# Side matmuls tied behind the main product in front of them, and the scans' three blocks in one burst

## The chip, the cores and the metric

The kernel runs on one core of one Trainium2 chip. The metric is the device time of one execution in microseconds (us); the time before is the median of 3 runs. TensorE (PE) multiplies and writes PSUM, VectorE (DVE) and ScalarE (ACT) do the elementwise work, GpSimd (POOL) issues small loads and clears tiles, SyncE (SP) issues the weight loads.

## The reference, cut to what matters

Two streams of 128 tokens (a prompt and a sample) go through two layers of a hybrid transformer block of width 2048. Only the parts around the change are kept here.

```python
def _mixer(h, p, ctx):
    u = h @ p['w_in']
    q, k, v, u_hy, u_rkv, w_dn, a_dn, g_dn = jnp.split(u, IN_SPLITS, axis=-1)
    att = attention(q, k, v)             # 12 heads, 4 kv heads; the sample also sees a cached context
    hy = _hyena(u_hy, p)                 # long convolution by FFT
    rw, S_fin = _rwkv(u_rkv, w_dn, a_dn, g_dn, p, S0)
    return concat([att, hy, rw]) @ p['w_out']

def _layer(x, cond, p, ctx):
    sh1, sc1, g1, sh2, sc2, g2 = silu(cond) @ ada_w + ada_b
    x = x + g1 * rmsnorm(_mixer(rmsnorm(x) * (1 + sc1) + sh1))
    h = rmsnorm(x) * (1 + sc2) + sh2
    return x + g2 * rmsnorm(square(relu(h @ p['mlp_w1'])) @ p['mlp_w2'])

def step(S, inp):                        # _rwkv: a scan over the 128 tokens, both directions, 12 heads
    sk = S @ kk_t
    S = S * w_t - outer(sk, kk_t * a_t) + outer(v_t, k_t)
    return S, S @ r_t
```

## The kernel before, in words

**Main products.** `ws` (L481) and `as_` (L503) multiply activations by weights streamed from HBM. `wload` (L211) loads a weight tile by SP, rounds it to a high part on ACT (L219) and takes the rest as a low part on DVE (L220); there are four raw tiles and three of each part. Each product is three matmuls (high by high, high by low, low by high): L495, L498, L499 in `ws`, L514, L517, L518 in `as_`. Both are generators and yield once for each k-step (128 rows of the weight), with the count of columns they streamed.

**Side work.** Attention, the hyena convolution and the RWKV recurrence are generators that `Side` holds. `run` (L1089) drives a main product: after each k-step it adds columns/6144 to `side.now` (0.5 for a 512-wide product, 0.375 for a 384-wide one), gives each generator credit at its rate, and lets a generator run on to its next yield when it has a whole credit and the number that it yielded last has passed on `side.now`. So the program text interleaves k-steps and side steps; `drain` runs what is left when an output needs it. The vectors of the adaptive modulation (`ada_vector`, L361, matmuls L374) are a third stream, driven by `ada_step`.

**Order on the engines.** The tile framework reorders: it dispatches each engine's instructions by program order among those that are ready in its own model of time. An engine then works through its queue strictly in that order. A side matmul whose turn in the program comes after a main product may thus stand ahead of it in PE's queue, where the model held the product's weights to be late.

**Attention** (L647) for each stream: transposes of keys (L686) and queries (L693), scores (L705), softmax on DVE and ACT (L708 to L718), transposes of the probabilities (L725), products with the values (L734). It yields 0.5 and `wa1` = 1.5 after its two halves of the scores, before the transposes. Its generator has the rate `ra` = 0.3. **Hyena** (L598): transposes (L612), spectra (L619, L620), and for each of four channel groups four matmuls back (L639, L640) and a yield.

**RWKV** works on 6 blocks of 128 channels in 2 batches of 3. A batch builds triangular matrices for each block (`rwkv_stage1`), sends their diagonal pieces through HBM (L937, L938, read back by SP at L956), inverts all at once by 30 steps on DVE (L964, L965; `rwkv_invert`), and then solves by blocks of 32 tokens in `rwkv_stage2` (L980): seven steps, alternately with the inverted diagonal (L1003) and with what lies off it (L1001). Each step does, for each of the three channel blocks in turn, 8 matmuls into one PSUM tile `sm`, two evictions (L1007, or L1009 and L1011) and a yield of `w5` = 0.25. There are three `sm` tiles for all side work.

Of the kernel before, what the change touches and what calls it, by code (L numbers as in the profile page):

```python
# [33 lines left out]
def _shape_constants():  # L34
# [56 lines left out]
    for k, v in c.items():  # L91
# [18 lines left out]
            ni=3, w2=0.5, w3=3, w4=2, w5=0.25, fill=8, b1=2, b2=5)  # L110
# [46 lines left out]

class Kern:
    def __init__(self, tc, es, A, O, opts=None):
# [6 lines left out]
        self.side = Side()  # L166
        self.adaq = deque()
# [56 lines left out]
    def setup(self):  # L224
# [17 lines left out]
        nc.tensor.transpose(ps[:, 0:32], th[:], self.ident[0:32, 0:32])  # L242
# [21 lines left out]
    def params(self, l):  # L264
# [34 lines left out]
        for i, gr in enumerate(groups):  # L299
# [3 lines left out]
            nc.tensor.transpose(ps[:, 0:n], rows[:], self.ident[0:n, 0:n])  # L303
# [151 lines left out]
    def norm(self, P, parts, isc, ish, act):  # L455
# [3 lines left out]
        for c in range(4):  # L459
            for g in range(2):  # L460
# [4 lines left out]
                for j in range(4):  # L465
                    nc.tensor.transpose(pv[:, j, :], xn[:, j * 128:(j + 1) * 128], self.ident)
# [14 lines left out]
    def ws(self, act, w, widths, ps):  # L481
# [21 lines left out]
    def as_(self, lhs, ks, w, ncol, ps):  # L503
# [3 lines left out]
        for i0 in range(0, len(ks), nk):  # L507
            hi, lo = self.wload(w[ks[i0] * 128:(ks[i0] + nk) * 128, :], nk, ncol)
            for kk in range(nk):
                first, last = i0 + kk == 0, i0 + kk == len(ks) - 1  # L510
                for g in range(2):
                    hh, hl = (a[:, g * 128:(g + 1) * 128] for a in lhs[ks[i0 + kk]])
                    o = ps[:, g * 512:g * 512 + ncol]
                    m = nc.tensor.matmul(o, lhsT=hh, rhs=hi[:, kk, :], start=first, stop=False)  # L514
# [35 lines left out]
    def hyena_filter(self, l):  # L550
# [16 lines left out]
        nc.tensor.matmul(ps[0:64, 0:128], lhsT=f1[:], rhs=self.cst("featt")[0:33, :], start=True, stop=True)  # L567
# [3 lines left out]
        nc.tensor.matmul(ps[0:64, 0:128], lhsT=f2[:], rhs=h1[:], start=True, stop=True)  # L571
# [5 lines left out]
        for q in range(2):  # L577
            ps = self.sm()
            nc.tensor.matmul(ps[:], lhsT=h2[:], rhs=f3[:, q * 512:(q + 1) * 512], start=True, stop=True)
            nc.vector.scalar_tensor_tensor(h[:, q * 512:(q + 1) * 512], dec[:, q * 512:(q + 1) * 512], 0.05, ps[:], op0=ALU.add, op1=ALU.mult)  # L580
            yield
# [8 lines left out]
        for i, (m, src) in enumerate((("cosm", hs), ("sinm", hd), ("cosn", hs))):  # L590
            ps = self.sm()
            nc.tensor.matmul(ps[:], lhsT=self.cst(m), rhs=src[:], start=True, stop=True)
# [5 lines left out]
    def hyena(self, l, P, hy):  # L598
# [11 lines left out]
        for j in range(4):  # L610
            for g in range(2):
                nc.tensor.transpose(pz[g][:, j * 128:(j + 1) * 128], z[j][:, g, :], self.ident)  # L612
            yield
        Y = []
        for g in range(2):
# [3 lines left out]
            nc.tensor.matmul(pa[:], lhsT=self.cst("cosm"), rhs=zt[:], start=True, stop=True)  # L619
            nc.tensor.matmul(pb[:], lhsT=self.cst("fb"), rhs=zt[:], start=True, stop=True)  # L620
# [14 lines left out]
        for j in range(4):  # L635
            ps = self.sm()
            for g in range(2):
                o = ps[:, g * 128:(g + 1) * 128]
                nc.tensor.matmul(o, lhsT=Y[g][0][:, j * 128:(j + 1) * 128], rhs=self.cst("ia"), start=True, stop=False)  # L639
                nc.tensor.matmul(o, lhsT=Y[g][1][:, j * 128:(j + 1) * 128], rhs=self.cst("ib"), start=False, stop=True)  # L640
# [6 lines left out]
    def attention(self, l, P, qk, v):  # L647
# [27 lines left out]
        for g in range(2):  # L675
# [7 lines left out]
            for i, kk in enumerate((kd, kc)[:g + 1]):  # L683
                ps = self.sm()
                for n in range(4):
                    nc.tensor.transpose(ps[:, n * 128:(n + 1) * 128], kk[:, n, :, :].rearrange("p r d -> p (r d)"), self.ident)  # L686
# [3 lines left out]
            for h0, hn in ((0, 4), (4, 2)):  # L690
                ps = self.sm()
                for j in range(hn):
                    nc.tensor.transpose(ps[:, j * 128:(j + 1) * 128], src[:, (h0 + j) * 128:(h0 + j + 1) * 128], self.ident)  # L693
# [4 lines left out]
            for b0, hpb in (((0, 4), (4, 2)), ((0, 2), (2, 2), (4, 2)))[g]:  # L698
                pes, pTs = [], []
                for par in range(2):  # L700
# [3 lines left out]
                    for j, h in enumerate(range(NH)[hsl]):  # L704
                        nc.tensor.matmul(ps[:, j * nk:(j + 1) * nk], lhsT=qT[o:o + 64, h // 2, :], rhs=kT[o:o + 64, h // 3, :], start=True, stop=True)  # L705
# [15 lines left out]
                for par in range(2):  # L721
                    ps = self.sm()
                    for j in range(hpb):
                        for i in range(g + 1):
                            nc.tensor.transpose(ps[:, j * nk + i * 128:j * nk + (i + 1) * 128], pes[par][:, j, i * 128:(i + 1) * 128], self.ident)  # L725
# [4 lines left out]
                for j in range(hpb):  # L730
                    for i in range(g + 1):
                        for par in range(2):
                            n = (2 * (b0 + j) + par) // 3
                            nc.tensor.matmul(po[64 * par:64 * par + 64, j * 128:(j + 1) * 128], lhsT=vs[i][:, n * 64:(n + 1) * 64],  # L734
# [37 lines left out]
    def rwkv_state(self, l, P, bt):  # L772
# [7 lines left out]
        for d in range(2):  # L780
            ps = self.sm()
            for b in range(3):
                nc.tensor.transpose(ps[:, b * 64:(b + 1) * 64], s[d][:, 2 * b:2 * b + 2, :].rearrange("p h k -> p (h k)"), self.ident[0:64, 0:64])
# [3 lines left out]
    def rwkv_kk(self, P, bt, k):  # L787
# [3 lines left out]
        for bi in range(3):  # L791
# [3 lines left out]
            nc.tensor.matmul(ps[0:6, 0:256], lhsT=self.cst("ones6")[:, 6 * bi:6 * bi + 6], rhs=sq[:], start=(bi == 0), stop=(bi == 2))  # L795
# [575 lines left out]
```

## Time and profile before

| | us |
|---|---|
| median of 3 runs | 2942.34 |
| the runs | 2932.66 to 2944.27 |
| the profiled execution, its own time | 2951.85 |
| its span, first to last instruction | 2950.1 |
| PE busy in the span | 2840.5 (96%) |
| DVE, ACT busy | 1652.6, 1231.1 |
| mean granted TensorE clock | 0.967 |

How to read the rows below. A row of instructions by line has the line, engine, operation, out<-in with its shape and count, then busy us and mean ns. A row of the timeline has start and duration in us, the engine, line, tiles, shape and the count that was merged; in brackets stands the idle time of the engine before it and what ended it. A matmul of fp32 data is two records in the trace, of the rounded type one. A row of a stretch has its start and end, its length, the busy us of PE, PEld, DVE, ACT and POOL with their counts, then the granted clock (1.00 is 2.4 GHz, 0.50 is 1.2 GHz), the share of the DMA engines that was busy, and GB/s. Matmuls overlap, so the time that one adds is read from the starts, not from the durations.

### The profile page before, as it was taken

The page shows a single profiled execution, that of the slowest core. Times are in us where ns is not written, and L with a number is a line of the kernel's source. Part 1 is how long each engine was busy: PE and PEld are TensorE (multiplying, and loading weights), DVE is VectorE, ACT ScalarE, POOL GpSimd, SP SyncE. Part 2 cuts the span into 40 slices and gives each one's busy share as a digit, 9 for nine tenths or more (in the row PEclk, how much of TensorE's full clock was granted, in tenths as well). Part 3 has the DMA queues.
Part 4 walks back from the last instruction along what each step waited for, and adds up shares of the span by engine and source line. Part 5 has one row for each costly group of instructions (what it writes and reads, how often), then busy time and mean ns, then how long its engine had stood idle before and what let it go on. Part 6 is the DMA issues. An engine that isn't in the chain of part 4 may idle for free.

```text
span 2950.1 us, 47852 instructions
## 1 busy us (share of the span) xinstructions
PE 2840.5 (96%) x19163; PEld 2330.7 (79%) x19163; DVE 1652.6 (56%) x2627; ACT 1231.1 (42%) x1870; POOL 177.7 (6%) x368
## 2 busy tenths in 40 slices
PE   6899999999999999999999999999879999999998
PEld 2586788766798797887876978887669989889896
DVE  1356666777644344444445576776775545555555
ACT  2254345434534343343335454453354444434343
POOL 0011101201000000000001111011000000000000
PEclk8899999999999999999999998997889999999999
DMA  9885575478888888888888744532455666666674
GB/s 341 308 300 195 187 257 158 140 263 282 296 278 293 276 287 274 297 279 280 300 318 274 227 124 124 145 92 88 131 195 164 184 189 186 187 191 186 188 238 153
DMA packets 326057, 654.56 MB, mean 222 GB/s; under 512 B 48581, under 2 KB 86030, under 8 KB 325707
## 3 DMA queue, kind: packets, MB, share of 16 engines
q1 hardware_dynamic: 311328, 610.88, 63.8%
q0 software_dynamic: 12928, 36.98, 3.7%
q10 hardware_dynamic: 1579, 3.64, 0.3%
q8 instruction: 150, 2.46, 0.3%
q14 instruction: 72, 0.59, 0.1%
HBM read 632.21 MB, written 19.20 MB: 221 GB/s over the span
## 4 chain that ended last, share of the span: by engine, by line
PE 86%; DVE 6%; DMA 4%; ACT 2%; issue 2%; SPq 0%; POOL 0%; DVEq 0%; ACTq 0%; POOLq 0%
PE mm L495 13%; PE mm L498 12%; PE mm L499 12%; PE mm L514 11%; PE mm L517 11%; PE mm L518 10%; PE ada L374 5%; PE sm L904 2%; DMA wa<-in_ada_w_dram 1%; PE sm L925 1%; PE sm L1003 1%; DVE wl L220 1%; PE sm L1018 1%; PE sm L1001 1%; DMA wr<-in_ada_w_dram 1%
## 5 line engine op out<-in xcount | busy, mean ns | idle before, releaser
L220 DVE TENSOR_TENSOR wl<-wr,wh 128x1024 fp32r<-128x1024 f32 (+1 forms) x784 | 928.9, 1186 | 929.7 <-ACT wh L219 900.3
L219 ACT CAST wh<-wr 128x1024 fp32r<-128x1024 f32 (+1 forms) x784 | 796.7, 1017 | 1163.2 <-PE mm L498 548.2
L495 PE MATMUL mm<-acth,wh 128*128 128x256 f32 (+1 forms) x3200 | 918.8, 287 | 9.9 <-ACT acth L476 8.3
L498 PE MATMUL mm<-actl,wh 128*128 128x256 f32 (+1 forms) x3200 | 908.5, 284 | 0.0
L499 PE MATMUL mm<-acth,wl 128*128 128x256 f32 (+1 forms) x3200 | 905.3, 283 | 2.4 <-DVE wl L220 2.4
L495 PEld LDWEIGHTS mm<-acth,wh 128*128 128x128 f32 (+1 forms) x3200 | 604.8, 189 | 54.7 <-issue 23.1
L499 PEld LDWEIGHTS mm<-acth,wl 128*128 128x128 f32 (+1 forms) x3200 | 605.6, 189 | 8.3 <-DVE wl L220 3.4
L498 PEld LDWEIGHTS mm<-actl,wh 128*128 128x128 f32 (+1 forms) x3200 | 603.7, 189 | 3.6 <-issue 2.5
L514 PE MATMUL mm<-wh,fh 128*128 128x512 f32 x1024 | 406.0, 396 | 0.0
L517 PE MATMUL mm<-wl,fh 128*128 128x512 f32 x1024 | 403.1, 394 | 0.8 <-DVE wl L220 0.8
L518 PE MATMUL mm<-wh,fl 128*128 128x512 f32 x1024 | 401.7, 392 | 0.0
L514 PEld LDWEIGHTS mm<-wh,fh 128*128 128x128 f32 x1024 | 192.2, 188 | 63.4 <-ACT wh L219 11.4
L518 PEld LDWEIGHTS mm<-wh,fl 128*128 128x128 f32 x1024 | 192.0, 188 | 45.3
L517 PEld LDWEIGHTS mm<-wl,fh 128*128 128x128 f32 x1024 | 192.3, 188 | 43.2 <-DVE wl L220 1.2
L374 PE MATMUL ada<-wa,cs 128*32 128x512 f32 x1280 | 183.1, 610 | 7.3 <-DMA wa<-in_ada_w_dram 7.3
L514 PE MATMUL mm<-wh,osh 128*128 128x512 f32 x256 | 107.9, 422 | 3.4 <-ACT osh L1172 3.4
L517 PE MATMUL mm<-wl,osh 128*128 128x512 f32 x256 | 103.9, 406 | 3.4 <-DVE wl L220 3.4
L518 PE MATMUL mm<-wh,osl 128*128 128x512 f32 x256 | 102.5, 400 | 0.0
L374 PEld LDWEIGHTS ada<-wa,cs 128*32 128x32 f32 x1280 | 35.5, 109 | 83.5 <-issue 55.3
L904 PE MATMUL sm<-rZR,rKB 64*128 64x256 f32 x384 | 82.3, 446 | 1.1 <-ACT rKBt L882 0.5
L514 PE MATMUL mm<-wh,acth 128*128 128x512 f32 (+1 forms) x192 | 74.3, 387 | 0.0
L517 PE MATMUL mm<-wl,acth 128*128 128x512 f32 (+1 forms) x192 | 68.9, 359 | 0.0
(323 smaller groups left out, 2619.5 us busy)
## 6 DMA issues: line engine op xcount, KB each, us to landing
wr<-in_mlp_w_dram SPq DMA_DIRECT2D x512, 512.0 KB
wa<-in_ada_w_dram SPq DMA_DIRECT2D x352, 512.0 KB
wr<-in_w_in_dram SPq DMA_DIRECT2D x96, 512.0 KB
wr<-in_w_in_dram SPq DMA_DIRECT2D x112, 384.0 KB
wr<-in_w_out_dram SPq DMA_DIRECT2D x64, 512.0 KB
wr<-in_ada_w_dram SPq DMA_DIRECT2D x32, 512.0 KB
gb<-gate POOLq DMA_DIRECT2D x16, 512.0 KB, 9.6
xd<-acc SPq DMA_DIRECT2D x24, 256.0 KB
```

The lines of the kernel that those rows point to most:

```text
L219: nc.scalar.copy(hi, raw)
L220: nc.vector.tensor_sub(lo, raw, hi)
L374: nc.tensor.matmul(ps[32 * j:32 * j + 32, :], lhsT=self.cs[:, kk, :], rhs=w[2 * (kk - k + 1) + j // 2][:, 512 * (j % 2):512 * (j % 2) + 51 ...
L495: m = nc.tensor.matmul(o, lhsT=h, rhs=hh, start=(k == 0 and b % 2 == 0), stop=False, skip_group_check=True)
L498: nc.tensor.matmul(o, lhsT=h, rhs=hl, start=False, stop=False, skip_group_check=True)
L499: nc.tensor.matmul(o, lhsT=lw, rhs=hh, start=False, stop=(k == KT - 1), skip_group_check=True)
L514: m = nc.tensor.matmul(o, lhsT=hh, rhs=hi[:, kk, :], start=first, stop=False)
L517: nc.tensor.matmul(o, lhsT=hh, rhs=lo[:, kk, :], start=False, stop=False)
L518: nc.tensor.matmul(o, lhsT=hl, rhs=hi[:, kk, :], start=False, stop=last)
L904: nc.tensor.matmul(ps[h][:, i * 256:(i + 1) * 256], lhsT=KB[hs, d, g, i, :], rhs=ZR[hs, d, g, :, :].rearrange("p i t -> p (i t)"), start=T ...
L925: nc.tensor.matmul(o[:, 64 * h:64 * h + 64], lhsT=R.MA[d][h][:, 0:128] if i == 0 else MY[h][:], rhs=vT[:, g, 64 * h:64 * h + 64], start=fi ...
L1001: nc.tensor.matmul(o, lhsT=LA[d][:, gh, qs[d]], rhs=G[:, d, gh, :], start=True, stop=True)
```

## The change

Two edits. First, a class `Beside`: `ws` and `as_` issue the first matmul of each product (L495, L514) through `te.main`, which keeps its name. Every matmul and transpose of the side work, of the norms and of the small setup steps (not those of the modulation, L335, L344, L374, L398) goes through `te.matmul` or `te.transpose`, which adds an edge without a semaphore: the instruction may not be placed ahead of that last main matmul in PE's queue. Second, in the solve each step first takes three `sm` tiles, issues the 24 matmuls of the three blocks, then the six evictions, and yields once, 3 x `w5`, with `w5` 0.4 in place of 0.25.

```diff
-            ni=3, w2=0.5, w3=3, w4=2, w5=0.25, fill=8, b1=2, b2=5)
+            ni=3, w2=0.5, w3=3, w4=2, w5=0.4, fill=8, b1=2, b2=5)
+class Beside:
+    def __init__(self, tc):
+        self.tc, self.last = tc, None
+    def main(self, *a, **k):
+        i = self.tc.nc.tensor.matmul(*a, **k)
+        self.last = i.ins.name
+        return i
+    def queue(self, i):
+        if self.last is not None:
+            self.tc.add_manual_dep(i.ins, self.last, mybir.DependencyInfo(mybir.DependencyClass.NoSync, mybir.DependencyReason.DATA),
+                                   reason="beside")
+        return i
+    def matmul(self, *a, **k):
+        return self.queue(self.tc.nc.tensor.matmul(*a, **k))
+    def transpose(self, *a, **k):
+        return self.queue(self.tc.nc.tensor.transpose(*a, **k))
...
-                    m = nc.tensor.matmul(o, lhsT=h, rhs=hh, start=(k == 0 and b % 2 == 0), stop=False, skip_group_check=True)
+                    m = self.te.main(o, lhsT=h, rhs=hh, start=(k == 0 and b % 2 == 0), stop=False, skip_group_check=True)
...
-                        nc.tensor.matmul(ps[:, j * nk:(j + 1) * nk], lhsT=qT[o:o + 64, h // 2, :], rhs=kT[o:o + 64, h // 3, :], start=True, stop=True)
+                        self.te.matmul(ps[:, j * nk:(j + 1) * nk], lhsT=qT[o:o + 64, h // 2, :], rhs=kT[o:o + 64, h // 3, :], start=True, stop=True)
...
             for first in (True, False)[it == 0:]:
+
+                pss = [self.sm() for b in B]
                 for bi, b in enumerate(B):
                     vT, KBt, G, Y, bv, LA = P.st[b]
-                    ps = self.sm()
                     for gh in range(4):
                         for d in range(2):
-                            o = ps[qs[d], gh * 64:(gh + 1) * 64]
+                            o = pss[bi][qs[d], gh * 64:(gh + 1) * 64]
...
+                for bi, b in enumerate(B):
+                    G = P.st[b][2]
                     for d in range(2):
-                        v = ps[qs[d], 0:256].rearrange("p (i v) -> p i v", i=4)
+                        v = pss[bi][qs[d], 0:256].rearrange("p (i v) -> p i v", i=4)
...
-                    yield self.o["w5"]
+                yield 3 * self.o["w5"]
```

## Rows read from the trace of the kernel before

**Rows 1.** The page, part 1: busy time of each engine.
```profile
PE 2840.5 (96%) x19163; PEld 2330.7 (79%) x19163; DVE 1652.6 (56%) x2627; ACT 1231.1 (42%) x1870; POOL 177.7 (6%) x368
```
**Rows 2.** The page, part 4: the chain that ended last, by engine.
```profile
PE 86%; DVE 6%; DMA 4%; ACT 2%; issue 2%; SPq 0%; POOL 0%; DVEq 0%; ACTq 0%; POOLq 0%
```
**Rows 3.** Timeline of PE, layer 0, around the prompt's attention.
```profile
333.92 0.60 PE L686 MATMUL sm<-const,akd 128*128 128x128 f32 x4
...
342.07 0.99 PE L725 MATMUL sm<-const,ape 128*128 128x128 f32 x4 [2.99 <-DVE ape L718]
...
349.58 0.58 PE L495 MATMUL mm<-acth,wh 128*128 128x256 f32 x1
...
351.21 0.58 PE L499 MATMUL mm<-acth,wl 128*128 128x256 f32 x1 [0.84 <-DVE wl L220]
```
**Rows 4.** Stretches: that detour in each layer, and the main products after the first.
```profile
333.92:349.58 15.66, 10.98 (x69) 7.73 (x67) 8.80 (x33) 7.72 (x28) 0.00 (x0) 0.77 0.10 41
1802.71:1818.84 16.13, 11.06 (x61) 8.49 (x59) 10.23 (x36) 7.52 (x27) 0.00 (x0) 0.62 0.00 1
349.58:356.10 6.52, 5.68 (x26) 5.39 (x26) 6.24 (x17) 2.09 (x4) 0.94 (x1) 0.51 0.52 156
```
**Rows 5.** Timeline of ACT in the same place.
```profile
334.56 0.59 ACT L687 COPY akT<-sm 128x512 f32<-128x512 f32 x1 [8.16 <-PE sm L686]
...
347.66 0.81 ACT L219 CAST wh<-wr 128x768 fp32r<-128x768 f32 x1
```
**Rows 6.** Timeline of SP's queue in the same place.
```profile
329.65 0.42 SPq L369 DMA_DIRECT2D wa<-in_ada_w_dram  x1
351.18 1.44 SPq L218 DMA_DIRECT2D wr<-in_w_in_dram  x2
```
**Rows 7.** Timeline of PE, layer 1: the transposes where main products stand between them.
```profile
1860.60 0.53 PE L725 MATMUL sm<-const,ape 128*128 128x128 f32 x2 [0.86 <-DVE ape L718]
```
**Rows 8.** Timeline of PE and DVE, layer 1, around the hyena products.
```profile
2067.36 0.48 PE L514 MATMUL mm<-wh,osh 128*128 128x512 f32 x1
2070.82 0.50 PE L517 MATMUL mm<-wl,osh 128*128 128x512 f32 x1 [2.97 <-DVE wl L220]
...
2066.46 0.19 DVE L964 TENSOR_TENSOR rkt<-rX 112x30 f32<-112x30 f32 x1
...
2069.55 1.22 DVE L220 TENSOR_TENSOR wl<-wr,wh 128x1024 fp32r<-128x1024 f32 x1
```
**Rows 9.** Stretches: those hyena products with the wait, and the scan's slow part.
```profile
2064.65:2070.82 6.17, 3.20 (x27) 2.84 (x25) 5.76 (x17) 3.91 (x5) 0.00 (x0) 1.00 0.00 0
2110.50:2130.90 20.40, 18.97 (x162) 13.18 (x162) 6.13 (x14) 2.86 (x6) 0.00 (x0) 0.50 0.25 71
```
**Rows 10.** Groups by line: the scans' matmuls and evictions, half of the inversion.
```profile
L1003 PE MATMUL sm<-rG,rXT 32*32 32x64 f32 x768 | 33.6, 228 | 2.0 <-DMA rXT<-rdout 2.0
L1001 PE MATMUL sm<-rG,rLA 128*32 128x64 f32 x576 | 24.3, 229 | 0.6 <-DVE rG L1007 0.6
L1007 DVE TENSOR_TENSOR rG<-rG,sm 32x256 f32<-32x256 f32 x72 | 30.0, 417 | 15.9 <-PE sm L1001 14.3
L965 DVE TENSOR_TENSOR rX<-rX,rkt 112x30 f32<-112x30 f32 (+14 forms) x120 | 39.6, 330 | 2.9
```
**Rows 11.** Timeline of PE: one scan block alone (layer 1), two in one (layer 0).
```profile
2145.36 0.64 PE L1001 MATMUL sm<-rG,rLA 128*32 128x64 f32 x16
...
2146.27 0.39 PE L517 MATMUL mm<-wl,osh 128*128 128x512 f32 x1
2146.50 0.40 PE L518 MATMUL mm<-wh,osl 128*128 128x512 f32 x1
...
2147.51 0.64 PE L1001 MATMUL sm<-rG,rLA 128*32 128x64 f32 x16
...
671.51 1.08 PE L1003 MATMUL sm<-rG,rXT 32*32 32x64 f32 x32
672.52 1.05 PE L374 MATMUL ada<-wa,cs 128*32 128x512 f32 x2
```

More of the change, by code (lines that the diff above doesn't have):

```diff
@@ L166, in __init__ @@
         self.side = Side()
+        self.te = Beside(tc)
         self.adaq = deque()
@@ L241, in setup @@
         ps = self.sm()
-        nc.tensor.transpose(ps[:, 0:32], th[:], self.ident[0:32, 0:32])
+        self.te.transpose(ps[:, 0:32], th[:], self.ident[0:32, 0:32])
         nc.vector.tensor_copy(self.cs[:, :, 0:2], ps[:, 0:32].rearrange("p (c k) -> p k c", c=2))
@@ L302, in params @@
             ps = self.sm()
-            nc.tensor.transpose(ps[:, 0:n], rows[:], self.ident[0:n, 0:n])
+            self.te.transpose(ps[:, 0:n], rows[:], self.ident[0:n, 0:n])
             pv = sb([128, n], F32, tag=f"pv{i}", bufs=2)
@@ L513, in as_ @@
                     o = ps[:, g * 512:g * 512 + ncol]
-                    m = nc.tensor.matmul(o, lhsT=hh, rhs=hi[:, kk, :], start=first, stop=False)
+                    m = self.te.main(o, lhsT=hh, rhs=hi[:, kk, :], start=first, stop=False)
                     if g == 0 and kk == 0:
@@ L591, in hyena_filter @@
             ps = self.sm()
-            nc.tensor.matmul(ps[:], lhsT=self.cst(m), rhs=src[:], start=True, stop=True)
+            self.te.matmul(ps[:], lhsT=self.cst(m), rhs=src[:], start=True, stop=True)
             H = sb([128, 512], F32, tag="hHs")
@@ L611, in hyena @@
             for g in range(2):
-                nc.tensor.transpose(pz[g][:, j * 128:(j + 1) * 128], z[j][:, g, :], self.ident)
+                self.te.transpose(pz[g][:, j * 128:(j + 1) * 128], z[j][:, g, :], self.ident)
             yield
@@ L618, in hyena @@
             pa, pb = self.sm(), self.sm()
-            nc.tensor.matmul(pa[:], lhsT=self.cst("cosm"), rhs=zt[:], start=True, stop=True)
-            nc.tensor.matmul(pb[:], lhsT=self.cst("fb"), rhs=zt[:], start=True, stop=True)
+            self.te.matmul(pa[:], lhsT=self.cst("cosm"), rhs=zt[:], start=True, stop=True)
+            self.te.matmul(pb[:], lhsT=self.cst("fb"), rhs=zt[:], start=True, stop=True)
             ya = sb([128, 512], F32, tag="hya")
@@ L813, in rwkv_stage1 @@
         for g in range(2):
-            nc.tensor.transpose(ps[:, g * 128:(g + 1) * 128], v[:, g, :], self.ident)
+            self.te.transpose(ps[:, g * 128:(g + 1) * 128], v[:, g, :], self.ident)
         vT = sb([128, 2, 128], F32, tag="rvT")
@@ L921, in rwkv_stage1 @@
                     if g == 1:
-                        nc.tensor.matmul(o, lhsT=ZR[:, d, 1, i, :], rhs=S0[:, d, :, :].rearrange("p h v -> p (h v)"), start=first, stop=False, skip_group_check=True)
+                        self.te.matmul(o, lhsT=ZR[:, d, 1, i, :], rhs=S0[:, d, :, :].rearrange("p h v -> p (h v)"), start=first, stop=False, skip_group_check=True)
                         first = False
                     for h in range(0 if (i, d) == (1, 0) else 2):
-                        nc.tensor.matmul(o[:, 64 * h:64 * h + 64], lhsT=R.MA[d][h][:, 0:128] if i == 0 else MY[h][:], rhs=vT[:, g, 64 * h:64 * h + 64],
+                        self.te.matmul(o[:, 64 * h:64 * h + 64], lhsT=R.MA[d][h][:, 0:128] if i == 0 else MY[h][:], rhs=vT[:, g, 64 * h:64 * h + 64],
                                          start=first, stop=True, skip_group_check=True)
```

52 lines of the change are left out of this document (26 added, 26 removed).

## The prediction

> **What bounds the kernel now.** The page comes first: PE is busy for 96% of the span, DVE for 56% and ACT for 42% [rows 1], and 86% of the chain that ended last is PE's [rows 2]. So time falls only where PE does less, where it waits less, or where its clock stays up. In the MLPs I found no PE idle time that this change touches. So I went through PE's timeline in the two mixers, and looked where side matmuls stand in a row with no main product between them.
>
> The clearest place is the prompt's attention, once in each layer. Its generator yields 0.5 and 1.5 between scores and transposes, and a k-step of a 384-wide product counts 0.375, so in the program two and four k-steps belong there. In PE's queue there is none: transposes, scores, transposes and value products stand together from 333.92 to 349.58, and PE waits there, longest for the softmax (2.99 us) [rows 3]. Layer 1 has the same from 1802.71 on [rows 4]. Were the weights of the overtaken products really late? In both stretches the DMA engines are nearly idle, at 0.10 and 0.00 [rows 4]. SP issues its last load at 329.65 and the next one at 351.18 [rows 6]: the raw tiles are full. ACT sat idle for 8.16 us until the first key transposes came, then worked on attention, and took up the next weight cast only at 347.66 [rows 5]. So the weights lay there; ACT's queue, in the order that follows PE's, stood before their cast. The granted clock falls to a mean of 0.77 and 0.62 in these stretches and is 0.51 for the main products behind the first [rows 4]. **That detour is the main thing to be won.**
>
> **Part 1, the order of the queue.** The edges carry no semaphore, so no engine gets a new wait from them. Only the place in PE's queue changes. No DMA is tied, and nothing is moved past one on SP's or POOL's queue by the edge itself; the softmax and the evictions on DVE and ACT go along because they read these matmuls.
>
> Attention, layer 0. The detour takes 15.66 us, of which PE is busy for 10.98 [rows 4]. At a mean clock of 0.77 some 46% of the stretch, 7.2 us, is at half speed, and nearly all of it is busy time after 342 [rows 3], so half of it, about 3.3 us, is the clock's. The work itself is 7.7 us. Cut into about six pieces among main products it pays for switching: 0.2 us each, worked out for the scans below, so 6 x 0.2 = 1.2 us. Saved: 15.66 - 7.7 - 1.2 = 6.8 us. Behind it the main products run for 6.5 us at half clock and lose 0.84 us to a late low part [rows 3, 4]; that is (6.5 - 0.84) / 2 + 0.84 = 3.7 us. Together 10.5 us. Layer 1, same steps: 16.13 us, 11.06 busy, three quarters of the stretch at half clock (0.62), so work of 6.5 us and switching of 1 us, saved 8.6 us, and some 2.4 us behind it: 11 us. Sum 21.5 us. Against it, the softmax latency does not vanish: where transposes already stand among main products PE still waited 0.86 us [rows 7]. I put two such waits on each layer, and take off 4 us. **Term: -17.5 us**, bounds -21.5 (no new wait) and -12 (every idle us of the detours, 4.7 and 5.1, comes back elsewhere).
>
> Hyena. Here the side work is a filler. From 2064.65 to 2067.36 PE does products of several channel groups with no k-step between, then L514, then waits 2.97 us for a low part [rows 8], because DVE works on the inversion from 2066.46 and splits the weights only at 2069.55 [rows 8]. Behind the edge these 2.7 us come after the wait, so PE stands still for almost all of 6.17 us, where its idle time is now 2.97 us [rows 9]. Layer 0 has half of it (two channel groups, about 1.8 us at the price of these). After so long a pause I expect the clock to fall; the nearest row of a fall, 20.4 us at 0.50 [rows 9], gives 10 us at most, nothing is the other end, and I take 3.5, nearer the short falls. The Trainium skill speaks against the change here: its page "TensorE: Matmul & The Clock Gate", in "Why this matters for your kernels", wants no long idle gaps between bursts of matmuls, as the clock halves. By that rule 3.5 to 10 us are lost here and not none; the rows of the detour agree that waits bring the half clock. **Term: +8 us**, bounds +2 and +14.
>
> Other side matmuls are where the program puts them, or ahead by a few k-steps without an idle gap; moving them costs nothing while main products, which fill PE now, cover them.
>
> **Part 2, the scans.** L1003 and L1001 have 768 and 576 records [rows 10], 16 for each block and step: 84 blocks, which become 28 bursts. A lone block and the six main matmuls of its k-step take 2.15 us (2145.36 to 2147.51); main matmuls follow each other at 0.23 us (2146.27 to 2146.50) [rows 11], six take 1.38, so the block costs 0.77 us. Its 16 records take some 0.44 to 0.57 of that, and 0.2 or more is for switching. Two blocks that stand together, 32 records, take 1.01 us (671.51 to 672.52) [rows 11]: the second adds 0.44 us. So three in a burst cost 0.77 + 2 x 0.44 = 1.65 us where three alone cost 2.31: 0.66 us for each of 28 steps, 18.5 us if every block were alone now. Some already stand together, as at 671.51, or beside the modulation's matmuls; in the first batch attention competes for the three `sm` tiles, and a burst may be split. I take two thirds. **Term: -12 us**, bounds -18.5 and -6.
>
> The Trainium skill ("TensorEngine Tiling (Array Packing)", "Key Properties") says that different tiles of the array load and multiply in parallel. By that rule the second and third block would be nearly free, and 28 x 0.88 = 24.6 us more would go. But the blocks of a step use the same rows and columns of the array, and the row's 0.44 us decides.
>
> In layer 1 the second scan runs at 0.50 for 20.4 us [rows 9], which costs 10 us; single blocks alternate there with single main matmuls. With three k-steps in a row between bursts the clock may come back sooner: between nothing and 6 us, I take **-3 us**.
>
> Pace: 21 yields of 0.25 fall on one k-step each; 7 yields of 1.2 fall on every third k-step of 0.5, again 21, and on every fourth of 0.375, 28. So a scan beside 384-wide products ends up to 7 k-steps later; most k-steps of the scans are 0.5, and I cost this at nothing while k-steps remain to cover it. At a drain it would show a step's latency, 1 to 2 us.
>
> **The sum.** -17.5 + 8 - 12 - 3 = -24.5 us. The profiled execution took 2951.85 us (a span of 2950.1), 9.5 us above the median, so it would take 2927; taken off the median of 2942.34 that is **2918 us**.
>
> **Rivals.** *A, the evictions become the wait (2930).* For: a step with L1001 now has six evictions on DVE at its end, 6 x 0.417 = 2.5 us [rows 10], and in the 4.2 us of three k-steps DVE also splits 1.5 weight tiles of 1.23 us; a wait of 1 us for each of the 12 such steps takes back 12 us. Against: it still fits, with nothing else on DVE.
>
> *B, the detour stays in another form (2938).* For: the attention was pulled ahead since the weights count as late in the order's model; the casts on ACT and DVE may still be queued late, and PE then waits instead. Then attention gives nothing, and the scans and hyena leave -12 + 8 = -4 us. Against: with attention tied, nothing that depends on PE can go before the casts.
>
> *C, slower (2965).* One mechanism: the inversion on DVE stands ahead of the split in the place of the detour, as it does at 2066.46 [rows 8]. One inversion is 2 x 39.6 / 4 = 20 us of DVE [rows 10]. PE's queue is full until 333.92. The detour costs 15.66 + 3.7 = 19.4 us now, of which attention's work is 8. So once PE's wait for the split and the clock that it loses pass 11.4 us (a wait of 5 us, with half clock behind it), the change loses there. With all the inversion ahead, begun near 329, the wait is some 15 us and the half clock 10: 15 + 8 + 10 - 19.4 = 13.6 us a layer, 27 in all, +8 for hyena, -12 for the scans: +23. Against: at 2066.46 only a part of it, 3.1 us, went ahead.
>
> **How the numbers follow.** The forecast has 0.62, A 0.13, B 0.12, C 0.13. The forecast's bounds add up to -44 and -4, so its own range is 2898 to 2938. To hold 8 in 10 the range goes on over A and B to 2945 and leaves out C. A measurement can tell about 0.5%, 14.7 us, from no change: faster is below 2927.6. Of the forecast seven eighths lie there, and four tenths of A: 0.60. Same: the rest of these, and B: 0.26. Slower: C and a little of the others: 0.14.
>
> **What would show it.** Right: L686 to L734 with main products between them; no L725 wait of 2 us or more; a granted clock near 1.00 from 330 to 356; the DMA engines at work there; L1003 and L1001 in runs of 48 records; a longer wait of L517 near 2070. Wrong: a PE wait for the low part (L220) or the cast (L219) of several us where the detour was, L1001 waiting on L1007 in most bursts, or a PE that is no less busy in the scans.

## The result, and the profile after

The changed kernel takes 2912.64 us (median of 8 runs, 2904.51 to 2927.32), the kernel before 2942.57 in the runs beside it: a ratio of 0.990, 95% interval 0.9879 to 0.9921. It is faster by 1.0%, about 29 us, and 2918 had been forecast. The profiled execution took 2905.5 us with a mean clock of 0.98. One kernel's executions lie some 10 us to either side of their median, so below a place counts where two profiles differ by more than that, or where a row shows the reason; the rest goes by the medians of many runs.

Part 1 of the page after, to be held against [rows 1]: the count of instructions is the same and PE is busy for 42 us less. The same work took less time on PE. The mean granted clock of the two executions is 0.967 and 0.980; over their spans that alone makes some 39 us (an estimate: 2950.1 x 0.033 less 2903.8 x 0.020). These two executions are 46 us apart, more than the medians.

```profile
PE 2798.7 (96%) x19163; PEld 2308.9 (80%) x19163; DVE 1646.6 (57%) x2627; ACT 1232.8 (42%) x1870; POOL 179.1 (6%) x368
```

**Attention.** PE's timeline where [rows 3] had the detour: the transposes of keys and queries have main products between them. Two k-steps of nine main matmuls lie between keys and queries, three between queries and scores, four ahead of the first transposes of the probabilities.

```profile
333.47 0.60 PE L179 MATMUL sm<-const,akd 128*128 128x128 f32 x4
333.82 0.36 PE L165 MATMUL mm<-acth,wh 128*128 128x256 f32 x1
...
336.05 0.82 PE L179 MATMUL sm<-const,aqk 128*128 128x128 f32 x6
336.62 0.37 PE L165 MATMUL mm<-acth,wh 128*128 128x256 f32 x1
```

(In the changed kernel every tied matmul has the line L176, every tied transpose L179, the first matmul of each main product L165; the line numbers behind the edit are 25 to 28 higher.) The stretches of that place in both layers, columns as in [rows 4]: PE has no idle time at all, the clock is full, and the DMA engines work, where they stood at 0.10 and 0.00.

```profile
318.00:350.00 32.00, 32.00 (x263) 27.97 (x263) 25.06 (x65) 14.22 (x35) 1.51 (x2) 1.00 0.82 274
1785.00:1815.00 30.00, 30.00 (x248) 28.51 (x247) 28.47 (x76) 16.29 (x40) 0.95 (x1) 1.00 0.54 151
```

Against the main products ahead of the detour, those behind it start 17.7 us earlier than before in layer 0 (the 1100th of PE's queue) and 17.4 us in layer 1 (the 8100th). Of that, 13.4 and 13.8 us are left 150 main matmuls further on, since attention's work must now be done between main products.

**The solves.** PE's timeline in the second solve of layer 1: one step is whole (48 records), the next is cut, 32 and 16 with a main product between.

```profile
2084.95 1.08 PE L176 MATMUL sm<-rG,rXT 32*32 32x64 f32 x32
2085.96 0.50 PE L165 MATMUL mm<-wh,osh 128*128 128x512 f32 x1
2086.39 0.64 PE L176 MATMUL sm<-rG,rXT 32*32 32x64 f32 x16
...
2091.10 1.53 PE L176 MATMUL sm<-rG,rLA 128*32 128x64 f32 x48
```

The 84 blocks stood in 69 stretches of PE's queue before, and stand in 41 now, where 28 were meant. That the order counts a block's tile or operand as late, and so places a main product ahead of it, is my reading and not shown.

**New waits.** From the list of waits (engine, tile, line, what it waited for: us in total, times, longest), with the softmax' row, which was 7.2 us in five waits before:

```profile
PE sm L176 <- DMA rXT<-rdout: 6.9, 1, 6.9
PE sm L176 <- ACT rsf L1057: 4.4, 1, 4.4
PE sm L179 <- DVE ape L743: 0.9, 1, 0.9
```

The first is the start of layer 1's second solve; the stretch that it is in has half clock behind it:

```profile
2066.00:2083.00 17.00, 9.16 (x94) 6.44 (x96) 5.64 (x13) 2.87 (x9) 0.16 (x1) 0.60 0.37 88
```

The second stands in the gap between two phases of layer 0's output product. On ACT the eviction `rsf` is queued behind a weight cast whose load landed late (ACT's timeline):

```profile
681.07 1.05 ACT L244 CAST wh<-wr 128x1024 fp32r<-128x1024 f32 x1 [3.31 <-DMA wr<-in_w_out_dram]
682.02 0.26 ACT L1057 COPY rsf<-sm 128x128 f32<-128x128 f32 x1
```

and PE waits for the eviction (PE's timeline):

```profile
682.33 3.67 PE L176 MATMUL sm<-rG,rLA 128*128 128x64 f32 x16 [4.37 <-ACT rsf L1057]
```

**Hyena.** The wait of 2.97 us for a low part [rows 8] is gone. The list of waits has one row of the line L542 (which was L517):

```profile
PE mm L542 <- DVE wl L245: 0.3, 1, 0.3
```

### The profile page after: what moved, and what is told of

Same layout as the page of the kernel before. It is cut to its first block, busy times and chain, and to the rows that moved or that the text cites. A ratio compares the mean times of both kernels' runs of the same rounds, so it can differ in the third digit from the quotient of the medians.

```text
span 2903.8 us, 47850 instructions
## 1 busy us (share of the span) xinstructions
PE 2798.7 (96%) x19163; PEld 2308.9 (80%) x19163; DVE 1646.6 (57%) x2627; ACT 1232.8 (42%) x1870; POOL 179.1 (6%) x368
## 5 line engine op out<-in xcount | busy, mean ns | idle before, releaser
L165 PE MATMUL mm<-acth,wh 128*128 128x256 f32 (+1 forms) x3200 | 922.0, 288 | 11.8 <-ACT acth L501 8.5
L165 PEld LDWEIGHTS mm<-acth,wh 128*128 128x128 f32 (+1 forms) x3200 | 603.6, 189 | 61.0 <-issue 25.2
L165 PE MATMUL mm<-wh,fh 128*128 128x512 f32 x1024 | 405.8, 396 | 0.0
L542 PE MATMUL mm<-wl,fh 128*128 128x512 f32 x1024 | 403.0, 394 | 0.0
L165 PEld LDWEIGHTS mm<-wh,fh 128*128 128x128 f32 x1024 | 192.2, 188 | 63.0 <-ACT wh L244 9.2
L542 PEld LDWEIGHTS mm<-wl,fh 128*128 128x128 f32 x1024 | 192.2, 188 | 42.5 <-DVE wl L245 0.4
L165 PE MATMUL mm<-wh,osh 128*128 128x512 f32 x256 | 106.4, 416 | 4.9 <-ACT osh L1200 3.4
L542 PE MATMUL mm<-wl,osh 128*128 128x512 f32 x256 | 101.9, 398 | 0.3 <-DVE wl L245 0.3
L176 PE MATMUL sm<-rZR,rKB 64*128 64x256 f32 x384 | 76.4, 419 | 1.4 <-DVE rLA L933 1.4
L165 PE MATMUL mm<-wh,acth 128*128 128x512 f32 (+1 forms) x192 | 74.4, 387 | 0.0
L542 PE MATMUL mm<-wl,acth 128*128 128x512 f32 (+1 forms) x192 | 68.8, 358 | 0.0
```

The source lines that it names most:

```text
L165: i = self.tc.nc.tensor.matmul(*a, **k)
L176: return self.queue(self.tc.nc.tensor.matmul(*a, **k))
L542: nc.tensor.matmul(o, lhsT=hh, rhs=lo[:, kk, :], start=False, stop=False)
```

## The experiments

Gains are given in us as the ratio's distance from 1 times the median of the kernel before (2943 to 2948), with the 95% interval of the ratio. The runs are called e1 to e12, by the numbers of the paragraphs.

**1 to 3. The two parts alone, and attention alone.** The first has all edges and the solve as before; the second the bursts and no edge; the third has edges on attention's matmuls only.

```diff
-            ni=3, w2=0.5, w3=3, w4=2, w5=0.25, fill=8, b1=2, b2=5)
+            ni=3, w2=0.5, w3=3, w4=2, w5=0.4, fill=8, b1=2, b2=5)
...
+                pss = [self.sm() for b in B]
...
-                    yield self.o["w5"]
+                yield 3 * self.o["w5"]
```

That is the second; the first and the third have, against the kernel before, such lines, the first everywhere and the third in attention and in `ws` and `as_` only:

```diff
-                    m = nc.tensor.matmul(o, lhsT=h, rhs=hh, start=(k == 0 and b % 2 == 0), stop=False, skip_group_check=True)
+                    m = self.te.main(o, lhsT=h, rhs=hh, start=(k == 0 and b % 2 == 0), stop=False, skip_group_check=True)
...
-                    nc.tensor.transpose(ps[:, j * 128:(j + 1) * 128], src[:, (h0 + j) * 128:(h0 + j + 1) * 128], self.ident)
+                    self.te.transpose(ps[:, j * 128:(j + 1) * 128], src[:, (h0 + j) * 128:(h0 + j + 1) * 128], self.ident)
```

> All edges of the change, with the solve as it was before (one block, two evictions, a yield of 0.25). Theory (two separate gains): the attention detours go in both layers, about -18 us each where they stood, and some of it returns as attention's work between main products; against before -17 to -21 us, some two thirds of the whole. Rival 1 (the edges do all of it, the bursts are split up by the competition for the three sm tiles and bring nothing): -28 to -32 us. Rival 2 (the edges only move the work about): -6 to +3 us.

> The three-block bursts with 3 x 0.4 and no edge at all; the detours stay in the queue (38 attention matmuls in a row in each layer). Theory: -9 to -13 us against before, and together with the run of the edges alone it adds up to the change's -30. Rival 1: -3 to +3 us. Rival 2 (the bursts do nearly all): -25 to -30 us.

> Edges for attention's matmuls alone, the solve and every other side matmul as before. Theory: all of the gain of the edges is the detours', so this is within 4 us of the run with all edges: -17 to -21 us against before. Rival (the edges in hyena, in the solve and in the stages ahead of it have a part): at least 8 us short of the run with all edges. The prediction's hyena term of +8 us, if it were real, would make this run 8 us better than the one with all edges.

Measured: all edges 0.9932 (0.9908 to 0.9956), -20 us; bursts alone 0.9936 (0.9912 to 0.9960), -19 us; attention's edges alone 0.9925 (0.9899 to 0.9950), -22 us. So each part has a gain of its own. The edges' is attention's: that the third is as good as the first leaves nothing that shows for the other edges. The bursts gave more than the theory said. The two gains would add to -39 and the change has -29; the difference is not larger than the intervals allow. Of the new waits above, the one for `rXT` is in the second run too (6.7 us) and so already in its -19. The one for `rsf` (4.4 us) is in neither, but the run of paragraph 12, which hasn't got it, is no faster than the change. So these waits don't account for the difference.

The run with all edges also shows what the hyena term had spoken of. PE's timeline at the start of layer 1's output product: five and a half us of waiting, where it was 2.97 [rows 8].

```profile
2044.68 0.50 PE L165 MATMUL mm<-wh,osh 128*128 128x512 f32 x1 [2.11 <-ACT wh L244]
2048.59 0.79 PE L542 MATMUL mm<-wl,osh 128*128 128x512 f32 x1 [3.40 <-DVE wl L245]
```

DVE's timeline there: the inversion stands ahead of the weight split.

```profile
2044.23 0.18 DVE L989 TENSOR_TENSOR rkt<-rX 112x30 f32<-112x30 f32 x1
...
2047.31 1.22 DVE L245 TENSOR_TENSOR wl<-wr,wh 128x1024 fp32r<-128x1024 f32 x1
```

Half clock begins 0.9 us before the second wait ends (the stretch):

```profile
2047.70:2054.50 6.80, 5.91 (x16) 4.85 (x17) 5.62 (x11) 0.82 (x1) 0.00 (x0) 0.50 0.55 184
```

In e3, where hyena has no edge, the wait is as it was before, and the clock stays up (PE's timeline, and the stretch):

```profile
2048.87 0.50 PE L542 MATMUL mm<-wl,osh 128*128 128x512 f32 x1 [2.99 <-DVE wl L245]
2040.00:2054.00 14.00, 11.01 (x57) 8.73 (x56) 12.60 (x29) 4.96 (x6) 0.00 (x0) 1.00 0.25 79
```

**4 and 7. The cause of the detour.** No edge, no burst; the small loads of the inversion leave SP's queue. In e4 these are all 18, in e7 only the eight loads of `rX`.

```diff
-                nc.sync.dma_start(X0[r0:r0 + 12, :].rearrange("i (s t) -> i s t", s=32), R.din[d, :, qs, qs])
+                nc.gpsimd.dma_start(X0[r0:r0 + 12, :].rearrange("i (s t) -> i s t", s=32), R.din[d, :, qs, qs])
```

> The kernel before, no edges, no bursts; only the 18 small loads and stores of each inversion leave SP's queue for POOL's (rX in, rXo out, rXT in). Theory of the cause: in the order's model these wait on SP's queue ahead of the weight loads, so the weights count as late and attention is pulled ahead; without them the attention detour is gone from PE's queue (no row of 38 attention matmuls), and the time is -12 to -21 us against before. Rival (the model holds the weights late for another reason, or POOL's slower queue takes the gain back by a later rXT): -5 to +5 us.

> The kernel before with nothing changed but the queue of the eight loads rX of each inversion, POOL's instead of SP's (the stores rXo and the loads rXT stay on SP's, other than in the run with all three moved). In PE's queue the attention detour is gone. Theory of the cause (the rX loads ahead of the weight loads on SP's queue make the weights late in the order's model, and the detour is all that the attention edges remove): -14 to -22 us against before, the same as the edges in attention alone (-22.8). Rival (where the detour goes, a wait for rX on POOL's queue or for the inversion comes): -5 to +8 us.

Measured: e4 1.0036 (1.0017 to 1.0055), +11 us; e7 0.9998 (0.9980 to 1.0016). The cause is shown, the price is not. In both the row of 38 attention matmuls is gone from PE's queue, without any edge, and the stretch of [rows 4] in e7 is as full as in the changed kernel:

```profile
318.00:350.00 32.00, 32.00 (x272) 28.63 (x271) 14.85 (x25) 11.59 (x19) 9.57 (x14) 1.00 0.89 298
```

So it was the `rX` loads on SP's queue, ahead of the weight loads, that made the weights look late to the order. But the gain was given back later. The inversion of layer 1's second batch now runs until the output product is in its second phase, and PE waits for `rXT`. PE's timeline in e7:

```profile
2104.10 0.81 PE L1003 MATMUL sm<-rG,rXT 32*32 32x64 f32 x6 [15.54 <-DMA rXT<-rdout]
```

and in e4, where the stores and loads of the result are on POOL's queue too:

```profile
2109.03 0.81 PE L1003 MATMUL sm<-rG,rXT 32*32 32x64 f32 x6 [17.59 <-DMA rXT<-rdout]
```

**5. Bursts held together.** The main product that follows a burst in the program may not stand ahead of its last matmul.

```diff
     def main(self, *a, **k):
         i = self.tc.nc.tensor.matmul(*a, **k)
+        if self.hold is not None:
+            self.tc.add_manual_dep(i.ins, self.hold, mybir.DependencyInfo(mybir.DependencyClass.NoSync, mybir.DependencyReason.DATA), reason="hold")
+            self.hold = None
...
+                self.te.hold = i.ins.name
                 for bi, b in enumerate(B):
                     G = P.st[b][2]
```

> The changed kernel, and each main product that follows a burst in the program may not be placed ahead of the burst's last matmul. So the 28 steps of the solve stand in 29 stretches of PE's queue (41 in the changed kernel, 69 before), each of three blocks. Theory (the bursts gain by fewer switches between main and small products, about 0.33 us for each stretch saved, and by the clock): 12 stretches fewer, 4 us, with the clock up to 10: -4 to -10 us against the changed kernel, -33 to -40 against before. Rival (bursts were split because a tile or an eviction was late; held together they make PE wait some 1 us each): +5 to +12 us against the changed kernel, -18 to -25 against before.

Measured: 0.9896 (0.9869 to 0.9924), -31 us: neither theory; no different from the change. All steps are whole (PE's timeline, layer 1's first solve), and the stretches are 29:

```profile
1833.38 0.81 PE L179 MATMUL sm<-rG,rXT 32*32 32x64 f32 x6 [2.75 <-DMA rXT<-rdout]
1835.50 2.76 PE L179 MATMUL sm<-rG,rXT 32*32 32x64 f32 x42 [1.31 <-DMA rXT<-rdout]
1845.19 1.53 PE L179 MATMUL sm<-rG,rLA 128*32 128x64 f32 x48
1852.31 1.53 PE L179 MATMUL sm<-rG,rXT 32*32 32x64 f32 x48
```

Why so little? Take every stretch of the solve that stands at full clock and without a wait, from the start of the second main matmul ahead of it to the start of the second one behind it, less the usual steps of the main matmuls (0.23 us for 512 columns, 0.12 for 256). The second one behind belongs to it, since the first one's step is longer than usual. In the kernel before it is 0.34 us, from the 2145.93 of this row to the 2146.27 of [rows 11] (PE's timeline, around the block at 2145.36):

```profile
2145.03 0.40 PE L518 MATMUL mm<-wh,osl 128*128 128x512 f32 x1
...
2145.93 0.50 PE L514 MATMUL mm<-wh,osh 128*128 128x512 f32 x1
```

One block costs 0.77 us (29 stretches before), two 1.21 (3 stretches after), three 1.66 (21 in this run): 0.45 us for each block and 0.32 for the switch. The 12 stretches saved are thus 3.8 us, and the first burst's waits for `rXT`, 4.06 us in these rows, are as much.

**6 and 8. The pace, faster.** The same with 3 x 0.33, a burst on every second 512-wide k-step; then also each step of the inversion tied on DVE behind the last weight split before it in the program.

```diff
-            ni=3, w2=0.5, w3=3, w4=2, w5=0.4, fill=8, b1=2, b2=5)
+            ni=3, w2=0.5, w3=3, w4=2, w5=0.33, fill=8, b1=2, b2=5)
```

and in e8 on top of it (`self.low` is the name of the last split in `wload`, `m` the first instruction of a step):

```diff
+        self.low = nc.vector.tensor_sub(lo, raw, hi).ins.name
...
+            self.tc.add_manual_dep(m.ins, self.low, mybir.DependencyInfo(mybir.DependencyClass.NoSync, mybir.DependencyReason.DATA), reason="low")
             if k % ni == 0:
                 yield self.o["wi"]
```

> The same with 3 x 0.33 in place of 3 x 0.4: a burst on every second k-step of a 512-wide product instead of every third. Theory: the solve of the first batch ends some 7 k-steps (10 us) earlier, and so does all that stands behind it in the same row of generators; the 6.9 us wait for rXT in layer 1 goes, and its half clock behind it: -5 to -12 us against the run with the bursts held together at 0.4. Rival (the prediction's A: six evictions, 2.5 us of DVE, and 1.5 splits of 1.2 us don't fit into two k-steps of 2.8 us, and PE waits for them at most bursts): +8 to +20 us against it.

> The run with bursts held together at 3 x 0.33, which lost 28 us, and in it each step of the inversion may not be placed on DVE ahead of the last weight split before it in the program. Theory (the mechanism of the prediction's slower rival: the inversion ahead of the split; there PE waited 8.3 us for the low part in layer 0 and 3.4 in layer 1, each with half clock behind it): those waits go, -12 to -20 us against the untied run, -4 to -7 per thousand against before. Rival (the tied inversion ends later and the first burst waits as much longer for rXT): -4 to +4 us against the untied run.

Measured: e6 0.9997 (0.9981 to 1.0012), e8 1.0012 (0.9997 to 1.0028): the whole gain of the change is lost, but not by the evictions. The list of waits of e6 has a single one of a burst for an eviction, 0.9 us, and 8.3 us at once for a low part. The wait for `rXT`, which e6's theory saw gone, is there in five places, 14.0 us together (9.5 in e5), with 5.1 us more for `rX`. What each of these is worth was not taken apart. DVE's timeline of e6 in layer 0: ten us of the inversion without a break stand ahead of the split.

```profile
585.98 0.18 DVE L992 TENSOR_TENSOR rkt<-rX 112x30 f32<-112x30 f32 x1
...
595.68 0.41 DVE L993 TENSOR_TENSOR rX<-rX,rkt 112x238 f32<-112x238 f32 x1
596.00 1.22 DVE L248 TENSOR_TENSOR wl<-wr,wh 128x1024 fp32r<-128x1024 f32 x1
```

and PE waits for it (PE's timeline):

```profile
597.27 0.79 PE L545 MATMUL mm<-wl,osh 128*128 128x512 f32 x1 [8.30 <-DVE wl L248]
```

This is the mechanism of the prediction's rival C, at another spot. I held it for overtaking, as in attention, and that fell: with the tie the same wait is there to the hundredth (PE's timeline of e8).

```profile
607.34 0.80 PE L545 MATMUL mm<-wl,osh 128*128 128x512 f32 x1 [8.30 <-DVE wl L248]
```

So the inversion stands there by the program. As I read `drain`, it runs all generators until attention's output is there; with the faster pace the first solve is over by then, and what `drain` runs meanwhile is the next batch's inversion. That reading was not tried by itself.

**9. The wait for `rXT`.** The changed kernel, with the first burst of layer 1's second solve 35 main matmuls later.

```diff
-        yield self.o["w4"]
+        yield self.o["w4"] + 5 * bt * l
```

> The changed kernel, with five units more between the load of rXT and the first burst, for the second batch of layer 1 alone: the first burst stands 35 main matmuls (8 us) later in PE's queue. Theory (the 6.9 us wait for rXT and the half clock behind it, 13.7 us long, are a loss that the bursts brought): -6 to -12 us against the changed kernel, -36 to -42 against before. Rival (three more bursts then stand at the end of the solve with no main product between, each behind its evictions, and give it back): -3 to +4 us against the changed kernel.

Measured: 0.9907 (0.9883 to 0.9930), -27 us; the rival. The wait is gone, and the time comes back at the end of the solve: between the 9000th and the 9300th main matmul this run takes 88 us and the changed kernel 104, between the 9300th and the 9500th 86 and 71. There the last bursts stand in a row, each behind the evictions of the one before (PE's timeline):

```profile
2118.99 1.53 PE L176 MATMUL sm<-rG,rLA 128*32 128x64 f32 x48 [1.40 <-ACT rG L1039]
2121.52 0.64 PE L176 MATMUL sm<-rG,rXT 32*32 32x64 f32 x16 [0.99 <-DVE rG L1035]
```

17 us of half clock follow, though PE is busy all the time (the stretch):

```profile
2124.00:2141.00 17.00, 16.93 (x103) 15.65 (x104) 5.91 (x18) 4.76 (x12) 2.69 (x4) 0.50 0.14 44
```

**10. The waits for the scaled keys.** The changed kernel, with the key transposes of the twelve blocks some two k-steps later.

```diff
             nc.scalar.activation(kf[d][:], KB[:, d, 0, :, :], AF.Copy, ...)
-            yield
+            yield (0, 0.75)[d]
```

> The changed kernel, with a yield of 0.75 between the scaled keys (rkf) and their transposes in each of the twelve blocks, so that the transposes stand some two k-steps later. Theory (the clock falls behind such waits: a wait of 1.8 us at 1982.8 is followed by 17 us of half clock): 8 us of waits in nine places go, and part of the half clock: -6 to -14 us against the changed kernel. Rival (the solve starts some six k-steps later in each batch and the end of the solve has as much more with nothing between): -3 to +6 us against the changed kernel.

Measured: 0.9997 (0.9977 to 1.0017): 28 us slower than the change, worse than the rival said. The waits did fall, from 8.1 to 2.8 us, and the half clock behind them too: in the profile there is none between 1609 and 2087, where the changed kernel has 20.5 us of it. Others grew (list of waits):

```profile
PE ada L399 <- DMA wa<-in_ada_w_dram: 16.9, 12, 3.9
PE mm L543 <- DVE osl L1201: 12.4, 2, 10.6
PE sm L179 <- ACT rkf L899: 2.8, 5, 1.4
```

As I read these rows, what stands behind the blocks in the same generator reaches the joints between the phases later, and PE has nothing but the modulation's matmuls there; the joints were not tried one by one.

**11. The pace alone.** The kernel before, blocks one by one, no edge, with `w5` 0.4.

```diff
-            ni=3, w2=0.5, w3=3, w4=2, w5=0.25, fill=8, b1=2, b2=5)
+            ni=3, w2=0.5, w3=3, w4=2, w5=0.4, fill=8, b1=2, b2=5)
```

> The kernel before with w5 at 0.4 in place of 0.25 and nothing else: blocks one by one, no edge. Theory (the bursts' gain of 19 us comes from three blocks standing together: fewer switches, worked out from the starts as some 0.2 us for each stretch saved, and a clock that stays up with three k-steps between bursts; the pace alone gives nothing): -4 to +6 us against before. Rival (the pace moves what stands behind the solve to a better place, and the bursts themselves give little): -10 to -20 us.

Measured: 0.9954 (0.9936 to 0.9973), -14 us; the rival. Most of what the bursts gave is there without a burst: 71 stretches, and 69 before. What is left for the bursts themselves, some 5 us, is a little less than 0.32 us for each stretch saved (71 less 45 in e2, 26 x 0.32 = 8.3); the intervals of the two runs overlap. In the profiled executions the gain lies in layer 1, between the 8900th and the 9000th main matmul, where the last blocks of the second batch are built. That stretch in the kernel before:

```profile
1986.90:2046.30 59.40, 55.42 (x260) 42.96 (x259) 37.07 (x87) 18.75 (x44) 8.08 (x21) 0.71 0.20 61
```

and in this run:

```profile
1984.00:2017.70 33.70, 31.57 (x205) 24.93 (x203) 27.73 (x60) 16.61 (x37) 6.43 (x15) 1.00 0.21 69
```

Some of the work has moved out (205 matmuls, not 260), the rest is the clock: 0.71 of 59.4 us is 17 us that full clock would not have taken. Why the clock stays up there, one execution doesn't settle.

**12. Bursts, and edges in attention alone.** The changed kernel, without the edges outside attention; so in hyena, in the stages of the recurrence, in the norms and in the setup:

```diff
-                self.te.transpose(pz[g][:, j * 128:(j + 1) * 128], z[j][:, g, :], self.ident)
+                nc.tensor.transpose(pz[g][:, j * 128:(j + 1) * 128], z[j][:, g, :], self.ident)
```

> The bursts, and edges for attention's matmuls alone; hyena, the stages ahead of the solve, the norms and the solve itself have none. Theory (attention is all that the edges give; the bursts and the attention edges share some 8 to 10 us that only one of them can give): -28 to -34 us against before, within 4 us of the change. Rival 1 (the edges elsewhere cost something in the full change, such as the 4.4 us wait for rsf in layer 0 with 10 us of half clock behind it): -36 to -42. Rival 2 (the edges elsewhere are needed): -20 to -25.

Measured: 0.9888 (0.9866 to 0.9909), -33 us, and a median of 2914.4 against the change's 2912.6. The edges outside attention neither give nor cost anything that can be measured; between the theory and the first rival the number doesn't decide. No kernel tried was faster than the change by more than its interval.

**The clock in all executions.** For each execution the span and its mean granted clock are on record. The span times what the clock lacks of 1 is an estimate of the time that full clock would not have taken (too much where PE waits at half clock). Over the 79 executions of the kernel before that stand beside these runs, the span spreads by 6.6 us (standard deviation) and what is left of it by 2.9: most of the spread is the clock's. The gains cut in the same way, as means against those 79, in us:

| | span | the clock's part | the rest |
|---|---|---|---|
| the change (8 executions) | -31 | -22 | -9 |
| e1, all edges (6) | -18 | -17 | -1 |
| e3, attention's edges (6) | -20 | -15 | -5 |
| e2, bursts with the new pace (6) | -17 | -16 | -2 |
| e11, the new pace alone (12) | -14 | -18 | +4 |

The 95% intervals are some 5 us to either side for the clock's part and 2 for the rest. So some three quarters of the change's gain is clock, and the whole of the pace's; the bursts' own part is the 6 us by which the rest of e2 lies below that of e11. Why the clock stays up more with the slower pace, none of these runs shows.

## Why the prediction was right, and where it was not

**Attention** (-17.5 us) was right in its mechanism and its size: all signs that it named are there, the edges there alone give -22 us with an interval of -15 to -30, and what made the weights look late is shown by moving the `rX` loads. Of the 21.5 us that it worked out, some 13 were clock (3.3 and 2.8 in layer 0, 4.5 and 2.4 in layer 1); e3 has 15. Of the two softmax waits that it put on each layer only one of 0.9 us came.

**Hyena** (+8 us) failed. The step was that the products of hyena come behind the wait at the output product, and that PE stands still for 6 us there. With the edges alone (e1) it does, for 5.5 us, and 6.8 us of half clock come with it; e3, with no edge on hyena, waits 2.99 us at full clock. By these rows that is some 6 us (2.5 and half of 6.8), but e1's median is only 2 us above e3's, and their intervals overlap. The Trainium skill's rule that the clock halves behind a long idle gap ("TensorE: Matmul & The Clock Gate", "Why this matters for your kernels") agrees with that run. But the prediction judged each part against the trace of before. In the full change the pace has moved the solve, and with it the inversion, away from that place: layer 1's second inversion starts behind the 9084th main matmul of PE's queue in the change, in e2 and in e11, and behind the 9072nd before and in e1 and e3. The runs with the bursts and with the pace alone have no wait of 2.97 us there either. So the longer wait near 2070, which the prediction named as a sign of being right, did not come. The two parts were not independent.

**The solves** (-12 us). The cost of a step was right: 0.77 us for a lone block, read from one row [rows 11], is the mean of 29, and three together take 1.66 where 1.65 was worked out. The count was not. From 84 blocks to 28 bursts there were 56 switches to save, two thirds of them were taken, and half went (69 stretches to 41): 28 x 0.32 = 9.0 us. What failed is the pace, put at nothing: alone it gives about 14 us. It was costed only by its own steps, that a solve ends a few k-steps later; what counted is that everything behind it in the same generator moves too, and that the clock stays up more. The two errors cancelled in part.

The Trainium skill's rule that different tiles of the array multiply in parallel ("TensorEngine Tiling (Array Packing)", "Key Properties") says nothing of the second and the third block, which use the tiles of the first: they cost 0.45 us each, as the row had said. Within a block, where the two directions use different tiles, the trace agrees with it: the records start in pairs, some 7 ns apart and 49 ns ahead of the next pair, while those of L1018, which use the whole array and have 64 columns too, mostly start 112 ns apart.

**The clock** (-3 us) of layer 1's second solve was 20.4 us at 0.50 [rows 9] and is 13.7 in the profile after, -3.4 us. The size is right, the reason not: the half clock there comes with the 6.9 us wait for `rXT` and not with the single blocks. In all executions the clock's part of the gain is far larger than this term, some 22 us; attention's term had some 13 us of clock in it, the pace none.

**The sum**, -24.5, is near -29 partly by luck: too little was given to the pace (nothing for some 14 us), too much was taken off for hyena (8 us for nothing that the change shows), and the parts add to more than the whole, for a reason that stays open.

**The rivals.** A, the evictions: not in the change, whose list of waits has no row of a burst waiting for one, and not at the faster pace either, where there is one of 0.9 us. B, the detour in another form: the rows of the place exclude it. C, the inversion ahead of the split: not at the detour. Its price is real, 8.3 us and half clock behind it, but what brings it about is the program's own order, by the pace, and not the edges.

## What to carry to other kernels

Where side matmuls stand in a row although the program spreads them, look for what makes the weights look late (here eight small loads on their queue), and tie the order where that is cheaper than moving the loads. A knob that delays one step of a chain moves all that is behind it: before calling it free, list which drains and which shared engine the later steps then fall on. And where waits stand at the joints between stages, taking one away is worth little until it is clear what arrives next at that joint; the runs 4, 7, 9 and 10 removed what they aimed at and gained nothing, and 10 lost all that the change had gained.

## What was not expected of the hardware

Half clock can come behind a short wait, in a stretch where PE looks busy. In the profile after, PE is busy for 10.2 of 12 us with one wait of 1.79 us for `rkf`, and then for all of 17 us at 0.51 (stretches of PE):

```profile
1975.00:1987.00 12.00, 10.21 (x68) 8.53 (x68) 11.59 (x19) 6.72 (x15) 4.19 (x7) 0.99 0.21 66
1987.00:2004.00 17.00, 17.00 (x56) 12.38 (x56) 8.32 (x23) 4.19 (x14) 0.75 (x1) 0.51 0.21 70
```

That is some 8 us behind a wait of 1.8, and e10, where of these waits one of 1.38 us is left in layer 1's second batch, has no half clock there. But such a wait is not enough by itself. The profile of e11 has one of 1.83 us for `rkf` at 2014.05, and the kernel before has the 2.97 us of [rows 8]; around the one and behind the other the clock is full (a stretch of each):

```profile
2012.00:2020.00 8.00, 5.88 (x32) 3.66 (x32) 7.51 (x20) 6.29 (x16) 0.00 (x0) 1.00 0.21 64
2070.80:2077.60 6.80, 6.78 (x29) 5.56 (x30) 6.57 (x13) 2.10 (x2) 0.00 (x0) 1.00 0.67 212
```

What decides between them was not tried. Such stretches sit in other places in nearly every kernel profiled here, and the clock makes most of the spread between executions of one kernel, as the table above shows.
